# A decoder trunk on one Trainium2 core: four PSUM banks for the first sums of each MLP, separate tiles for the gate weights, and eight ways to begin a unit

## The chip, the cores and the metric

One core of one Trainium2 chip runs the whole program in one launch. The metric is the device time of that core in microseconds, from launch to end; smaller is better. Engine names are those of the profile: PE (matmul) with PEld (its weight loads), DVE (vector), ACT (scalar), POOL (GpSimd) and SP, whose queue issues all the DMAs.

## What is computed

Two layers over 256 tokens of width 2048. Layer 0 mixes by a gated linear recurrence, layer 1 by dilated attention; behind each stands an MLP with a squared ReLU. Every sublayer is normalized first and added to its input.

```python
for i in range(2):
    h = rmsnorm(x, mix_norm[i])
    if i == 0:
        x = x + rglru_block(h, w_in, conv_w, conv_b, w_a, b_a, w_x, b_x, lam, w_out)
    else:
        x = x + dilated_attention(h, w_qkv, w_o)
    h = rmsnorm(x, mlp_norm[i])
    x = x + square(relu(h @ w1[i])) @ w2[i]          # w1: 2048 x 8192, w2: 8192 x 2048
return rmsnorm(x, final_norm)

# rglru_block: xb, gb = split(h @ w_in); xb = causal conv of 4 taps
# r, i = sigmoid(block_diag(xb, w_a)), sigmoid(block_diag(xb, w_x))     10 blocks of 256 x 256
# a = exp(-8 r softplus(-lam)); h_t = a_t h_(t-1) + sqrt(1 - a_t^2) xb i; out = (h * gelu(gb)) @ w_out
```

All of it is float32, and the matmuls are done in fp32r: each operand is cut into a high part and the rest, and a product is three matmuls, high by high, high by low, low by high.

## The kernel before, in words

**Units.** The weights come in units of 128 x 2048 floats, 1 MB each (`unit`, L65), in one list. A DMA brings a unit into a `raw` tile (three buffers), ACT copies it to fp32r, which is its high part `whi` (`cut_hi`, L108; three buffers), and DVE subtracts to get `wlo` (`cut_lo`, L113; three buffers). The gates of the recurrence are units of half the width, 128 x 1024, in the same tiles. The tiles of one name are a ring: a new one takes the buffer of the third before it, and its writer waits until PE has read that.

**The order.** The work is a list of items, each the matmuls on one unit. The main loop (L916 to L926) runs it: before item `i` it issues loads up to unit `i+5`, `whi` up to `i+2` and `wlo` up to `i+2` (`before_unit`, L124); then come the item's matmuls, then `whi` of `i+3` (`behind_unit`, L130), and then what earlier items have asked for so many items later (`after`, L161): reading the sums, the next transposes, the activations. Each engine runs its own instructions strictly in this order.

**The recurrence.** For each of ten blocks there are four units of w_in, two for the recurrent branch and two for the other, and the gate unit of the block before, which stands behind the first of them; I call these five a turn. `stand_w` (L245) does a unit: sixteen slices of weights stand in PE and 256 tokens of `xT` move, three matmuls a slice: `whi` by the high tokens, `whi` by the low tokens, `wlo` by the high tokens. So a unit is 48 matmuls of 256 columns. Its sums go to a PSUM bank `acc` (four of them). `xb_done` reads them and runs the convolution on DVE, in block 1 partly on POOL; `conv_split` gives `chl`, the moving operand of the gate (`gate_run`, L373, 24 matmuls into two banks `g`); sigmoid, tanh, exp, square root, scan and split to `aT` follow over the next items.

**The MLP.** It goes by eight parts of 1024 hidden columns. The first matrix has eight units in a part, `j` = 0, 4, 1, 5, 2, 6, 3, 7 in this order, each done by `stand_w` into one of two banks `g`; `u_done` (L481) reads the bank on DVE with `rstdB`, the norm's factor, and the square and its split follow. For the second matrix the tokens and the columns are halved, and the product of a 2 x 2 block is done with seven products instead of eight, which is what the sums `qT`, `q` of weights and `sw`, `sT` of tokens are for. It works with 512 columns, in banks `acc` and `tr`. `ORDER` (L49) mixes the two: while part p has its second matrix, the units of part p+1 come in at the places "w", one between each two or three products, and `sums_of_tokens` runs behind each item.

**Part 0** has no part before it. `plan_start` does units 0 and 4 on the slices of the first three chunks of `xT`, and then on the fourth, since that is ready last; `plan_first` (L525) then does units 1, 5, 2, 6, 3, 7 on end. The factor `rstdB` takes longer: `rstd_rows` (L235) transposes it on PE behind unit 4, and ACT copies it, behind the `whi` that stand ahead of it.

Each layer is a scope with tiles of its own (`lru`); `wts`, `perm` and `psum` live through all of them.

Of the kernel before, what the change touches and what calls it, by code (L numbers as in the profile page):

```python
# [10 lines left out]
F32 = mybir.dt.float32  # L11
F32R = mybir.dt.float32r
# [5 lines left out]
S = 256  # L18
# [7 lines left out]
KD = D // 128  # L26
KR = DR // 128
NCH = D // 512
UW = 2048
# [12 lines left out]
HI_BUFS = 3  # L42
# [3 lines left out]
LOOK_LO = 2  # L46
LOOK_HI = 3
GROUPS = range(7)
ORDER = ("b11", "w", "b21", "s", "w", "t1", "w", "t2", "b22", "w", "s", "w", "t3", "w", "s", "w", "t4", "w", "s")  # L49


@with_exitstack
def trunk(ctx: ExitStack, tc: tile.TileContext, a: dict, out: bass.AP):
    nc = tc.nc
    P = 128

    perm = ctx.enter_context(tc.tile_pool(name="perm", bufs=1))
    wts = ctx.enter_context(tc.tile_pool(name="wts", bufs=1))
    psum = ctx.enter_context(tc.tile_pool(name="psum", bufs=1, space=bass.MemoryType.PSUM))
# [3 lines left out]
    units = []  # L63

    def unit(ap, width=UW):  # L65
        units.append({"ap": ap, "width": width})
        return len(units) - 1
# [6 lines left out]
    raw, split = {}, {}  # L74
# [14 lines left out]
    def make(i):  # L89
        if "load" in units[i]:  # L90
            units[i]["make"]()
            raw[i] = [(slice(0, UW), units[i]["source"]())]

    def new_hi(i):
        split[i] = (wts.tile([P, UW], F32R, name="whi", bufs=HI_BUFS),)

    def new_lo(i):
        split[i] += (wts.tile([P, UW], F32R, name="wlo", bufs=3),)

    def hi_piece(i, n):  # L100
        s, r = raw[i][n]
# [6 lines left out]
    def cut_hi(i):  # L108
        new_hi(i)
        for n in range(len(raw[i])):  # L110
            hi_piece(i, n)

    def cut_lo(i):  # L113
        new_lo(i)
        for n in range(len(raw[i])):
            lo_piece(i, n)
        del raw[i]
# [18 lines left out]
    def item(u, fn):  # L136
        items.append((u, fn))
# [21 lines left out]
    lru = Scope()  # L159

    def after(n, fn, *args):  # L161
        later.setdefault(now[0] + n, []).append((fn, args))

    def mm(o, l, r, start, stop):
        nc.tensor.matmul(o, l, r, start=start, stop=stop, skip_group_check=True)  # L165
# [23 lines left out]
    def xT(k):  # L189
        return state["xT", k // 4][:, k % 4, :]  # L190
# [51 lines left out]
        state["rstdB"] = rb  # L242


    def stand_w(ps, u, ks, w_at, first, last):  # L245
        hi, lo = split[u]
        for j, k in enumerate(ks):
            x = xT(k)
            s = slice((w_at + j) * 128, (w_at + j + 1) * 128)
            mm(ps, hi[:, s], x[:, 0:256], first and j == 0, False)  # L250
            mm(ps, hi[:, s], x[:, 256:512], False, False)
            mm(ps, lo[:, s], x[:, 0:256], False, last and j == len(ks) - 1)

    def stand_x(acc, u, get, ks, first, last, ts=range(NT)):
        hi, lo = split[u]
# [9 lines left out]
    def acc_tile():  # L265
        return psum.tile([P, 512], F32, name="acc", bufs=4)

    accs = {}
# [162 lines left out]
    def plan_rec():  # L431
        def proj(h, j, g):
            u = unit(a["w_in"][(KR if g else 0) + 2 * h + j])

            done = gb_done if g else xb_done
            if u < len(first):
                first[u] = (done, h, j)
                return

            def run():  # L440
                ps = acc_tile() if u > len(first) else psum.tile([P, 512], F32, name="g", bufs=2)
                stand_w(ps[:, :S], u, range(KD), 0, True, True)
                after(0, done, h, j, ps)
            item(u, run)
# [36 lines left out]
    def u_done(p, j, ps):  # L481
# [8 lines left out]
        after(1, u_low, t, uu)  # L490
        if h == 1 and p in GROUPS:
            after(1, waiting.append, (p, k))
# [31 lines left out]
    def plan_mlp(w1, w2, done):  # L524
        def plan_first(p, j):  # L525
            u = unit(w1[8 * p + j])

            def run():
                accs["u", p, j] = psum.tile([P, 512], F32, name="g", bufs=2)
                stand_w(accs["u", p, j][:, :S], u, range(KD), 0, True, True)  # L530
                after(0, u_done, p, j, accs.pop(("u", p, j)))
            item(u, run)

        def plan_start():
            us = [unit(w1[j]) for j in (0, 4)]
            for at, ks in enumerate((range(0, 12), range(12, 16))):
                for u, j in zip(us, (0, 4)):
                    def run(u=u, j=j, ks=ks, at=at):
                        if at == 0:
                            accs["u", 0, j] = psum.tile([P, 512], F32, name="g", bufs=2)  # L540
                        stand_w(accs["u", 0, j][:, :S], u, ks, ks[0], at == 0, at == 1)
                        if at == 1:
                            after(1 if j == 0 else 0, u_done, 0, j, accs.pop(("u", 0, j)))
                    item(u, run)
# [69 lines left out]
        for p in range(8):  # L614
            if p == 7 and done is final_done:
                item(None, load_g)
            if p < 7:
                nxt = iter([(p + 1, j) for j in (0, 4, 1, 5, 2, 6, 3, 7)])
            plain = [(n, h) for n in range(2 if p in GROUPS else 0, NCH) for h in range(2)]
            g = plan_group(p, 0) if p in GROUPS else {}  # L620
            for what in (ORDER if p in GROUPS else ("s", "w") * 8):
                if what == "w":
# [168 lines left out]
    first = [None] * 4  # L791
# [30 lines left out]
    for n in range(NCH):  # L822
        xg[n] = new_xg(n)
        rs = [wts.tile([P, UW], F32, name="raw", bufs=RAW_BUFS) for _ in range(3)] if n == 0 else rs
        for h in range(2 if n == 0 else 1):
            w = 2 if n == 0 else 4
            nc.sync.dma_start(xg[n][:, h * w:(h + 1) * w, :], a["xT"][:, 4 * n + h * w:4 * n + (h + 1) * w, :])
            for i in range(3):
                if n or i == 0:
                    s = slice(n * 512 + h * w * 128, n * 512 + (h + 1) * w * 128)  # L830
                elif h:
                    s = slice(0, 512)
# [5 lines left out]
        for h in range(2 if n == 0 else 1):  # L838
            w = 2 if n == 0 else 4
            for k in range(h * w, (h + 1) * w):  # L840
                nc.scalar.activation(t[:, k, 0:256], xg[n][:, k, :], AF.Identity, scale=pcol("mix0", 4 * n + k))
            for k in range(h * w, (h + 1) * w):
                nc.vector.scalar_tensor_tensor(t[:, k, 256:512], xg[n][:, k, :], pcol("mix0", 4 * n + k),  # L843
                                               t[:, k, 0:256].bitcast(F32), op0=OP.mult, op1=OP.subtract)
            for i in range(3):
                if n == 0 and h == 0:
                    new_hi(i)
                    new_lo(i)
                for at, (s, _) in enumerate(raw[i]):
                    if s.stop == n * 512 + (h + 1) * w * 128:  # L850
                        hi_piece(i, at)
                        lo_piece(i, at)
                        if s.start == 0:
                            accs["first", i] = acc_tile()
                            first[i] += (accs["first", i],)
                        ks = range(s.start // 128, s.stop // 128)
                        stand_w(accs["first", i][:, :S], i, ks, ks[0], s.start == 0, n == NCH - 1)
# [13 lines left out]
    for n in range(NCH):  # L871
        s = slice(n * 512, (n + 1) * 512)
# [15 lines left out]
    ps = psum.tile([P, 2, S], F32, name="tr", bufs=2)  # L888
# [23 lines left out]
    for at in range(len(items) - 1, -1, -1):  # L912
        u = items[at][0]
# [86 lines left out]
```

## Time and profile before

| | |
|---|---|
| time, median of 3 runs | 2189.44 us (2188.41 to 2190.64) |
| profiled execution, its own time | 2186.37 us |
| its span, first to last instruction | 2184.6 us |
| granted TensorE clock, mean | 0.995 |
| matmuls recorded | 13602 |
| read from HBM | 409.39 MB, 188 GB/s over the span |
| recurrence, MLP 0, attention, MLP 1 begin at | 5, 389, 1087, 1476 us |

A page gives each engine's busy time as a share of the span; matmuls are pipelined, and one record is longer than the distance to the next. So I read distances of starts. In a timeline a row is start, length, engine, line, operation, tiles written and read, shape, count, and in brackets the idle time before it and what ended it. In the list of waits a row is who waited for whom, total us, how many times, the longest. In the chain of waits a row is start, length and what the end of the program then hung on. Rows that group several instructions last from the first one's start to the last one's end.

### The profile page before, as it was taken

The numbers are of one execution on the slowest core, as the hardware profiler recorded it, in microseconds if no ns is written. First come the engines' busy times: TensorE is split into PE (matmuls) and PEld (weight loads), VectorE is DVE, ScalarE is ACT, GpSimd is POOL, SyncE is SP. The second block draws the span as 40 slices with busy tenths as digits, with TensorE's granted clock in tenths as the row PEclk, the third lists the DMA queues.
The fourth block names the chain that finished last, engine by engine and source line by source line (L and its number), as shares of the span: only waits on it lengthen the run. The fifth ranks groups of instructions, "written<-read, shape, count | busy, mean of one in ns | idle before, by whom it ended". The sixth has DMA issues, their size and how long they took to land.

```text
span 2184.6 us, 32102 instructions
## 1 busy us (share of the span) xinstructions
PE 2150.0 (98%) x13602; PEld 1944.2 (89%) x13602; DVE 1602.2 (73%) x1748; ACT 1166.2 (53%) x1261; POOL 81.3 (4%) x42
## 2 busy tenths in 40 slices
PE   7999999999999999999999999999999999999997
PEld 7999988999999999999888888889999999999996
DVE  8888865688888888787655555556888878887875
ACT  5777755554554555445545544555545544544543
POOL 2222100000000000000000000000000000000002
PEclk9999999999999999999999999999999999999999
DMA  6655565455465455554554444454564554545543
GB/s 220 213 190 190 183 222 180 174 203 221 138 248 189 177 195 207 185 223 163 179 198 156 172 174 173 157 191 161 206 231 144 222 213 154 218 187 193 212 175 134
DMA packets 61712, 413.56 MB, mean 189 GB/s; under 512 B 6784, under 2 KB 7168, under 8 KB 13440
## 3 DMA queue, kind: packets, MB, share of 16 engines
q1 hardware_dynamic: 61568, 411.51, 51.8%
q8 instruction: 106, 1.74, 0.3%
q14 instruction: 38, 0.31, 0.0%
HBM read 409.39 MB, written 2.10 MB: 188 GB/s over the span
## 4 chain that ended last, share of the span: by engine, by line
PE 80%; DVE 12%; ACT 5%; issue 2%; POOL 0%; DMA 0%; SPq 0%; DVEq 0%; ACTq 0%
PE acc L165 47%; PE g L165 27%; DVE wlo L106 7%; PE tr L165 4%; ACT whi L102 3%; DVE q L564 1%; ACT sT L181 1%; DVE xT L843 0%; DVE c L349 0%; DVE sT L182 0%; PE tr L205 0%; DVE aT L495 0%; DVE sw L506 0%; PE tr L664 0%; PE g L672 0%
## 5 line engine op out<-in xcount | busy, mean ns | idle before, releaser
L102 ACT ACTIVATE whi<-raw 128x2048 fp32r<-128x2048 f32 (+3 forms) x358 | 657.1, 1838 | 570.5 <-PE acc L165 313.9
L106 DVE TENSOR_TENSOR wlo<-raw,whi 128x2048 fp32r<-128x2048 f32 (+3 forms) x358 | 792.0, 2216 | 212.4 <-ACT whi L102 212.4
L165 PE MATMUL g<-xT,whi 128*128 128x256 f32 x4128 | 732.9, 281 | 5.8 <-DVE uu L486 5.8
L165 PEld LDWEIGHTS g<-xT,whi 128*128 128x128 f32 x4128 | 638.0, 188 | 15.2 <-DVE uu L486 6.3
L165 PE MATMUL g<-xT,wlo 128*128 128x256 f32 x2064 | 580.4, 281 | 2.1 <-DVE wlo L106 2.1
L165 PE MATMUL acc<-whi,aT 128*128 128x512 f32 x1840 | 580.5, 390 | 0.0
L165 PEld LDWEIGHTS acc<-whi,aT 128*128 128x128 f32 x1840 | 345.4, 188 | 69.6
L165 PEld LDWEIGHTS g<-xT,wlo 128*128 128x128 f32 x2064 | 395.3, 192 | 4.6 <-DVE wlo L106 4.6
L165 PE MATMUL acc<-wlo,aT 128*128 128x512 f32 x920 | 358.3, 389 | 0.0
L165 PE MATMUL acc<-whi,xT 128*128 128x512 f32 x768 | 245.9, 396 | 0.0
L165 PE MATMUL acc<-xT,whi 128*128 128x256 f32 x1248 | 223.5, 283 | 6.3 <-ACT whi L102 5.8
L165 PEld LDWEIGHTS acc<-wlo,aT 128*128 128x128 f32 x920 | 172.8, 188 | 33.5
L102 ACT ACTIVATE whi<-q 128x2048 fp32r<-128x2048 f32 x56 | 107.2, 1914 | 177.0 <-DVE q L564 137.8
L165 PEld LDWEIGHTS acc<-xT,whi 128*128 128x128 f32 x1248 | 195.0, 194 | 6.9 <-ACT whi L102 6.1
L165 PE MATMUL acc<-xT,wlo 128*128 128x256 f32 x624 | 178.2, 286 | 9.3 <-DVE wlo L106 9.0
L165 PEld LDWEIGHTS acc<-whi,xT 128*128 128x128 f32 x768 | 144.3, 188 | 30.7
L165 PE MATMUL acc<-wlo,xT 128*128 128x512 f32 x384 | 150.4, 392 | 0.0
L106 DVE TENSOR_TENSOR wlo<-q,whi 128x2048 fp32r<-128x2048 f32 x56 | 128.2, 2289 | 19.0 <-ACT whi L102 19.0
L165 PEld LDWEIGHTS acc<-xT,wlo 128*128 128x128 f32 x624 | 121.0, 194 | 12.0 <-DVE wlo L106 12.0
L102 ACT ACTIVATE whi<-qT 128x2048 fp32r<-128x2048 f32 x28 | 53.7, 1916 | 132.7 <-DVE qT L564 132.7
L106 DVE TENSOR_TENSOR wlo<-qT,whi 128x2048 fp32r<-128x2048 f32 x28 | 64.2, 2293 | 47.8 <-ACT whi L102 47.8
L165 PEld LDWEIGHTS acc<-wlo,xT 128*128 128x128 f32 x384 | 72.2, 188 | 15.1
(172 smaller groups left out, 1917.3 us busy)
## 6 DMA issues: line engine op xcount, KB each, us to landing
raw<-in_w SPq DMA_DIRECT2D x214, 1024.0 KB, 4.8
raw<-in_w_qkv SPq DMA_DIRECT2D x48, 1024.0 KB, 4.8
q<-in_w SPq DMA_DIRECT2D x42, 1024.0 KB, 6.9
raw<-in_w_in SPq DMA_DIRECT2D x35, 1024.0 KB, 4.8
raw<-in_w_out SPq DMA_DIRECT2D x20, 1024.0 KB, 4.8
raw<-in_w_o SPq DMA_DIRECT2D x16, 1024.0 KB, 4.8
raw<-in_w_g SPq DMA_DIRECT2D x10, 512.0 KB, 3.5
raw<-in_w_in SPq DMA_DIRECT2D x11, 256.0 KB, 6.1
```

The lines of the kernel that those rows point to most:

```text
L102: nc.scalar.activation(split[i][0][:, s], r, AF.Copy)
L106: nc.vector.tensor_sub(split[i][1][:, s], r, split[i][0][:, s].bitcast(F32))
L165: nc.tensor.matmul(o, l, r, start=start, stop=stop, skip_group_check=True)
L181: nc.scalar.activation(hi_out, src, AF.Copy)
L564: nc.vector.tensor_add(q[to], q[a], q[b])
```

## The change

Three things.

First, in part 0 of each MLP the sums of all eight units go to the four banks `acc` instead of the two banks `g`. The other parts keep `g`.

Second, the gates' halves have tiles of their own, `ghi` and `glo`, 128 x 1024, two buffers each, in the layer's own pool. `whi` and `wlo` keep three buffers each, which the gates no longer use.

Third, `stand_w` takes a way to begin, and `plan_first` picks it by `j`. A tuple of widths cuts the unit's first matmul (high weights by high tokens) into so many pieces of these widths, each a matmul with the same weights; "low" puts `wlo` by the high tokens first in every slice; "other" begins the unit with the low tokens and takes the high ones second. `plan_start` passes none, so units 0 and 4 of part 0 begin as before.

```diff
+BEGIN = {0: (), 4: (128, 128), 1: (64, 192), 5: (192, 64), 2: (32, 224), 6: (64, 64, 128), 3: "low", 7: "other"}
...
+    def cut_tile(i, name, bufs):
+        width = units[i].get("width", UW)
+        if width < UW:
+            return lru.tile([P, width], F32R, name="g" + name, bufs=2)
+        return wts.tile([P, UW], F32R, name="w" + name, bufs=bufs)
+
     def new_hi(i):
-        split[i] = (wts.tile([P, UW], F32R, name="whi", bufs=HI_BUFS),)
+        split[i] = (cut_tile(i, "hi", HI_BUFS),)
...
-    def stand_w(ps, u, ks, w_at, first, last):
+    def stand_w(ps, u, ks, w_at, first, last, begin=()):
+
         hi, lo = split[u]
         for j, k in enumerate(ks):
             x = xT(k)
             s = slice((w_at + j) * 128, (w_at + j + 1) * 128)
-            mm(ps, hi[:, s], x[:, 0:256], first and j == 0, False)
-            mm(ps, hi[:, s], x[:, 256:512], False, False)
-            mm(ps, lo[:, s], x[:, 0:256], False, last and j == len(ks) - 1)
+            parts = [(hi, 0, 0, 256), (hi, 0, 256, 512), (lo, 0, 0, 256)]
+            if begin == "low":
+                parts = parts[2:] + parts[:2]
+            elif begin == "other" and j == 0:
+                parts = [parts[1], parts[0], parts[2]]
+            elif begin and j == 0:
+                at, cuts = 0, []
+                for n in begin:
+                    cuts.append((hi, at, at, at + n))
+                    at += n
+                parts = cuts + parts[1:]
+            for n, (w, o, c0, c1) in enumerate(parts):
+                opens = first and j == 0 and n == 0
+                mm(ps[:, o:o + c1 - c0], w[:, s], x[:, c0:c1], opens, last and j == len(ks) - 1 and n == 2)
...
-                accs["u", p, j] = psum.tile([P, 512], F32, name="g", bufs=2)
-                stand_w(accs["u", p, j][:, :S], u, range(KD), 0, True, True)
+                accs["u", p, j] = acc_tile() if p == 0 else psum.tile([P, 512], F32, name="g", bufs=2)
+                stand_w(accs["u", p, j][:, :S], u, range(KD), 0, True, True, BEGIN[j])
...
-                            accs["u", 0, j] = psum.tile([P, 512], F32, name="g", bufs=2)
+                            accs["u", 0, j] = acc_tile()
```

On PE, at the end of unit 4 of part 0 and the start of unit 1, the rows were these (`tr<-con,rs` are the transposes of the norm's factor, the rows below them unit 1):

```order
L165 MATMUL g<-xT_4024,whi 128x256 x2
L165 MATMUL g<-xT_4024,wlo 128x256
L238 MATMUL tr<-con,rs 128x128 x2
L165 MATMUL g<-xT_3601,whi 128x256 x2
L165 MATMUL g<-xT_3601,wlo 128x256
L165 MATMUL g<-xT_3601,whi 128x256 x2
L165 MATMUL g<-xT_3601,wlo 128x256
```

They are now these, in the numbering of the changed file:

```order
L173 MATMUL acc<-xT_4024,whi 128x256 x2
L173 MATMUL acc<-xT_4024,wlo 128x256
L246 MATMUL tr<-con,rs 128x128 x2
L173 MATMUL acc<-xT_3601,whi 128x64
L173 MATMUL acc<-xT_3601,whi 128x192
L173 MATMUL acc<-xT_3601,whi 128x256
L173 MATMUL acc<-xT_3601,wlo 128x256
L173 MATMUL acc<-xT_3601,whi 128x256 x2
L173 MATMUL acc<-xT_3601,wlo 128x256
```

The bank is another, and the first matmul of unit 1 is two, of 64 and 192 columns. Nothing else moved on PE but such pieces, and the order of the three matmuls in units 3 and 7.

On ACT, in a turn of the recurrence, with the semaphores that each row waits for (`whi<-raw` are the high parts of coming units, the ACT_TABLE_LOAD and `r<-g` open the gate's sigmoid), it was:

```order
L102 ACTIVATE whi<-raw 128x2048 [waits DMAHW6_49,PE_49]
L181 ACTIVATE aT_2351<-i 128x256 [waits DVE_49]
L181 ACTIVATE aT_2354<-i 128x256
L368 ACTIVATE gw<-gb 128x512 [waits DVE_49,Pool_49]
L102 ACTIVATE whi<-raw 128x2048 [waits DMAHW7_49,PE_49,Activation_49]
L392 ACT_TABLE_LOAD
L392 ACTIVATE r<-g,par 128x256 x2
```

And now:

```order
L110 ACTIVATE whi<-raw 128x2048 [waits DMAHW6_49,PE_49]
L189 ACTIVATE aT_2351<-i 128x256 [waits DVE_49]
L189 ACTIVATE aT_2354<-i 128x256
L388 ACTIVATE gw<-gb 128x512 [waits DVE_49,Pool_49]
L110 ACTIVATE whi<-raw 128x2048 [waits DMAHW7_49,PE_49]
L412 ACT_TABLE_LOAD [waits PE_49]
L412 ACTIVATE r<-g,par 128x256 [waits Activation_49]
```

The instructions and their order are the same on ACT, DVE, POOL and SP. What moved is the waiting: both `whi` shown still wait for PE, but each for the end of the unit one before, since the gate no longer stands in their ring; and the wait for the gate's own end now stands at the table load behind the second `whi`. The `ghi` of a gate waits for its DMA alone.

More of the change, by code (lines that the diff above doesn't have):

```diff
@@ L92, in make @@
             raw[i] = [(slice(0, UW), units[i]["source"]())]
+    def cut_tile(i, name, bufs):
[3 more added lines that the diff above has]
+        return wts.tile([P, UW], F32R, name="w" + name, bufs=bufs)
     def new_hi(i):
-        split[i] = (wts.tile([P, UW], F32R, name="whi", bufs=HI_BUFS),)
+        split[i] = (cut_tile(i, "hi", HI_BUFS),)
     def new_lo(i):
-        split[i] += (wts.tile([P, UW], F32R, name="wlo", bufs=3),)
+        split[i] += (cut_tile(i, "lo", 3),)
     def hi_piece(i, n):
```

## The prediction

> **What bounds the kernel now.** I read the page first: the span, and which engine is busy all the time.
>
> ```profile
> span 2184.6 us, 32102 instructions
> PE 2150.0 (98%) x13602; PEld 1944.2 (89%) x13602; DVE 1602.2 (73%) x1748; ACT 1166.2 (53%) x1261; POOL 81.3 (4%) x42
> ```
>
> PE is the bound, so time goes only where PE waits or where its matmuls come slower than they could. The list of waits of PE says what the waits are worth:
>
> ```profile
> PE acc L165 <- DVE wlo L106: 9.0, 9, 3.1
> PE g L165 <- DVE uu L486: 5.8, 2, 2.9
> PE g L165 <- DVE wlo L106: 2.1, 12, 0.2
> ```
>
> All waits together are some 23 us, 1%. The second figure is how often. The two on uu stand at the start of part 0 of each MLP; PE's timeline there:
>
> ```profile
> 400.99 0.38 PE L238 MATMUL tr<-con,rs 128*128 128x128 f32 x2
> 404.29 0.50 PE L165 MATMUL g<-xT,whi 128*128 128x256 f32 x2 [2.91 <-DVE uu L486]
> 1488.30 0.38 PE L238 MATMUL tr<-con,rs 128*128 128x128 f32 x2
> 1491.60 0.50 PE L165 MATMUL g<-xT,whi 128*128 128x256 f32 x2 [2.92 <-DVE uu L486]
> 1492.11 0.63 PE L165 MATMUL g<-xT,whi 128*128 128x256 f32 x2
> 1495.31 0.43 PE L165 MATMUL g<-xT,whi 128*128 128x256 f32 x2
> ```
>
> The third unit wants a bank of `g`, both are held by units 0 and 4, and these are read only when rstdB is there. From 1492.11 to 1495.31 fifteen matmuls take 3.20 us, 0.213 each, half the usual pace: PE came back cold. After the first MLP's wait it did not.
>
> The second thing is pace. The chain of waits, with stretches of the same kind of matmul:
>
> ```profile
> 136.45 16.39 PE acc L165 x142
> 237.12 16.99 PE acc L165 x142
> 404.29 32.93 PE g L165 x288
> 484.33 5.55 PE g L165 x47
> 489.90 1.93 ACT whi L102
> 491.85 2.29 DVE wlo L106
> 496.84 2.28 DVE wlo L106
> 510.24 2.30 DVE wlo L106
> 512.58 5.50 PE g L165 x46
> 685.18 5.68 PE g L165 x46
> ```
>
> The same 142 matmuls take 16.39 or 16.99 us: there is a quick and a slow pace, 4.2 ns a matmul apart, 0.20 us on a unit of 48. A stretch keeps its pace. The last two rows are the same unit of two parts, each behind a wait, one quick, one slow; so how a unit begins decides, and I cannot see by which rule. Nearly all units between 512-column work are slow, as at 484.33 (5.55 for 47; the quick 32.93 for 288 is 5.37 for 47).
>
> The same rows show that from 489.90 to 512.58 the chain is not PE's: it runs over ACT and DVE from the end of unit 2 to the `wlo` of unit 7, where PE waits:
>
> ```profile
> 512.00 0.40 PE L165 MATMUL g<-xT,whi 128*128 128x256 f32 x2
> 512.58 0.38 PE L165 MATMUL g<-xT,wlo 128*128 128x256 f32 x1 [0.18 <-DVE wlo L106]
> ```
>
> The third matmul would have started at 512.24 (two at 0.118), and starts 0.34 later. What units 6 and 3 gain or lose up to 0.34 is therefore hidden.
>
> **Part 0 in four banks.** Unit 1 no longer waits for uu; it starts when the two transposes are through, 0.25 us behind 400.99 and 1488.30: 404.29 - 401.24 and 1491.60 - 1488.55, 3.05 each, -6.1. Its weights are there. Unit 5 is next late:
>
> ```profile
> 399.66 3.71 ACT L102 ACTIVATE whi<-raw 128x2048 fp32r<-128x2048 f32 x2 [1.30 <-PE g L165]
> 401.61 2.29 DVE L106 TENSOR_TENSOR wlo<-raw,whi 128x2048 fp32r<-128x2048 f32 x1 [2.27 <-ACT whi L102]
> ```
>
> Those are its halves (DVE, then 403.90), wanted at 401.24 + 5.65 = 406.9: 3.0 us to spare. Banks: units 1 and 5 take those that the last w_out chunk has left, unit 2 that of unit 0, read by 404.29 (that is what the wait was for) and wanted at 401.24 + 2 x 5.65 = 412.5. The cold stretch goes with the wait: fifteen matmuls at 0.213 instead of 0.114, -1.5. The Trainium skill, page "TensorE: Matmul & The Clock Gate", section "What's actually happening", lets the clock halve after an idle window that runs free of the kernel; by that rule either, both or neither wait could find it, and this profile has one of two. The credit for the timed runs is thus 0 to 3.0. On the other side, the six units behind the wait ran quick; if half of them are slow now, that is six times 0.20, +1.2. Five more matmuls per part 0 come in (below), +1.1.
>
> **Gate tiles of their own.** In the first stage PE waits once a turn on `wlo`:
>
> ```profile
> 110.60 0.39 PE L165 MATMUL acc<-xT,whi 128*128 128x256 f32 x2
> 111.29 0.39 PE L165 MATMUL acc<-xT,wlo 128*128 128x256 f32 x1 [0.29 <-DVE wlo L106]
> 111.51 0.40 PE L165 MATMUL acc<-xT,whi 128*128 128x256 f32 x2
> 102.43 1.92 ACT L102 ACTIVATE whi<-raw 128x2048 fp32r<-128x2048 f32 x1 [3.52 <-PE acc L165]
> 104.68 0.76 DVE L182 TENSOR_TENSOR aT<-i,aT 128x256 fp32r<-128x256 f32 x2 [1.82 <-ACT aT L181]
> 108.95 5.58 DVE L106 TENSOR_TENSOR wlo<-raw,whi 128x2048 fp32r<-128x2048 f32 x2
> PE acc L165 <- DVE wlo L106: 1.8, 6, 0.3
> ```
>
> (PE, ACT, DVE, and PE's waits from 110 to 270.) The matmul at 111.29 was due at 110.83, and the next came 0.22 behind it instead of 0.11: 0.57 lost. It goes back to ACT at 102.43, which waited for a whi buffer until its unit had ended; aT stood behind it on ACT, DVE waited 1.82 for aT, and the `wlo` at 108.95 came that much late. When the gate takes none of the three buffers, this `whi` waits for the unit before: 3.52 us go at its head, DVE's 1.82 with them, and the first of the two `wlo` runs from 107.13 to 109.4, 1.4 before it is wanted. DVE is next late, but in time. Six waits at 0.57: -3.4. The wait of 2.4 us near 81 stays: ACT there stands behind the Pool engine, which the change leaves alone.
>
> ```profile
> PE acc L165 <- DVE wlo L106: 2.4, 1, 2.4
> 63.29 0.63 ACT L181 ACTIVATE chl<-c 128x512 fp32r<-128x512 f32 x1 [4.76 <-POOL c L347]
> ```
>
> The wait for the gate's end moves to the table load in front of the sigmoid, which needed it anyway.
>
> **The beginnings.** Cutting adds one matmul to units 4, 1, 5, 2 and two to unit 6; 94 in all. No fp32r matmul under 256 columns is in the trace. Two neighbours bound its price:
>
> ```profile
> 393.05 1.04 PE L205 MATMUL tr<-con,xc 128*128 128x128 f32 x8
> 393.84 0.48 PE L165 MATMUL g<-xT,whi 128*128 128x256 f32 x2
> 1162.89 0.39 PE L671 MATMUL g<-qk 128*128 128x128 f32 x2
> 1163.12 0.60 PE L672 MATMUL g<-qk 128*128 128x256 f32 x2
> 1163.55 0.49 PE L695 MATMUL tr<-con,s 128*128 128x128 f32 x3
> ```
>
> Eight transposes of 128 columns need 0.79, 0.10 each, though half as wide as 256: each has its weight load. Two pieces for one matmul then cost 2 x 0.10 - 0.118 = 0.08 more, or 0.118 if a piece is no cheaper than the whole; I take 0.11. Fp32 matmuls, two records each, take 0.23 for 128 and 0.43 for 256 columns. If narrow fp32r went at that rate, an opening of 256 columns would cost 0.43 instead of 0.118, +0.31 a unit. Nothing rules out a gain either, since the opening may bring the quick pace (-0.20). I take the transposes: like these matmuls they are one record each. On the path stand, in 14 parts, units 4, 1, 5, 2: 56 x 0.11 = +6.2, and half of them quick, 28 x -0.20 = -5.6. Units 6 (0.22), 3 and 7 lie under the 0.34; if that cover is gone, 14 x 0.22 = 3.1. Unit 3 wants `wlo` first: that is the one of 496.84, ready at 499.1; by PE's order unit 3 starts behind unit 6 and 24 matmuls of 512 columns, 13 us after 490, so it has some 4 us to spare. The Trainium skill, same page, section "Back-to-back issue gap", gives 81 ns for a pair of load and matmul at 128 columns; the transposes here need 100. By 81 the 66 pieces on the path cost 5.3 instead of 7.3, and the sum would be 2 us lower.
>
> **Sum.** -6.1 - 1.5 + 1.2 + 1.1 - 3.4 + 6.2 - 5.6 = -8.1. The profiled execution took 2186.37 (span 2184.6 and 1.8 around it), 3.1 below the median of 2189.44; I carry the difference over: 2189.44 - 8.1 = **2181.3**. Its own range, with the cold credit at 0 to 3.0 and a quarter to three quarters of the units quick (2.8 either way): 2176 to 2186.
>
> **Rivals.**
> - Narrow fp32r pieces run at the fp32 rate. Then 56 + 8 units cost 0.31 instead of pieces at 0.11: 19.8 instead of 7.3, sum +4.4, 2193.8; with no unit turned quick (+5.6) 2199.4. It decides from 0.24 us a unit on: without the pieces the sum is -15.4, over 64 units. For it: the L671 and L672 rows, the only ones with as few columns that are no transposes. Against: at 256 columns fp32r (0.118) is not run the fp32 way (0.43), and no row says that it is below. Chance 0.28, half of it slower by more than can be told from no change.
> - The first stage loses its quick pace. Its waits also reset it: 136.45 was quick behind one, 237.12 slow. Without waits it keeps what it has after 89 us: seven turns of 192 matmuls slow, 7 x 192 x 0.0042 = +5.6, sum -2.5, 2186.9. Chance 0.18.
> - No beginning turns a unit quick: +5.6 and +1.2 in part 0, sum -1.3, 2188.1. Chance 0.12. All do: -5.6 - 1.2, 2174.5, chance 0.06.
> - The gate tiles do not do what they are for: DVE itself is late and the six waits stay. Sum -4.7, 2184.7. Chance 0.06.
>
> **Numbers.** The forecast has 0.30. A measurement of this kernel tells about 0.2% (4.4 us) from no change. Faster by more: 0.28 of the forecast, 0.06 of all quick, 0.03 of the gate tiles, 0.03 of the first rival, 0.08 of the slow first stage and of no unit quick: 0.48. Slower by more: 0.14 of the first rival, and 0.06 for its mixtures with a slow first stage: 0.20. The rest, 0.32. The range takes in all quick nearly and the first rival up to its upper half: 2174 to 2198.
>
> **What would show it.** In the profile after: no wait on uu in the list; the chain's 404.29 row starting near 401; the six `wlo` waits after 105 us gone, and the rows of 142 still 16.4; the starts of a unit 4 or 1 cut, 0.11 and not 0.2 to 0.4 apart; units of 48 at 5.45 or 5.65 by their place, the same in all parts. It is wrong if narrow pieces take more than twice 0.118, if uu or a bank of `acc` still holds unit 1, or if a new wait stands at unit 5 or 2 of part 0.

## The result and the profile after

| | before | after |
|---|---|---|
| time, median of 3 runs | 2189.44 us (2188.41 to 2190.64) | 2174.44 us (2173.93 to 2174.55) |
| ratio, 95% interval | | 0.9932 (0.9913 to 0.9952) |
| profiled execution, its own time | 2186.37 us | 2173.93 us |

15.0 us less, where 8.1 had been forecast: the sign is right and the size half. The page after, span and engines, and the list of PE's waits, its first two rows (only one more, of 1.3, is over a microsecond):

```profile
span 2172.1 us, 32279 instructions
PE 2143.5 (99%) x13696; PEld 1938.4 (89%) x13696; DVE 1601.9 (74%) x1748; ACT 1168.5 (54%) x1261; POOL 80.6 (4%) x42
```

```profile
PE acc L173 <- DVE wlo L114: 8.1, 4, 2.7
PE acc L173 <- ACT whi L110: 6.3, 2, 5.8
```

PE issues 94 matmuls more and is busy 6.5 us less, so its matmuls come quicker. The 5.8 us on uu are gone, and of the nine waits on `wlo` into `acc` four are left. The start of part 0 of the first MLP, PE's timeline (the row of three is the piece of 64, the one of 192 and the next matmul of 256):

```profile
395.07 0.38 PE L246 MATMUL tr<-con,rs 128*128 128x128 f32 x2
395.21 0.59 PE L173 MATMUL acc<-xT,whi 128*128 128x64 f32 x3
395.64 0.28 PE L173 MATMUL acc<-xT,wlo 128*128 128x256 f32 x1
```

Unit 1 begins 0.14 us behind the transposes, where it had stood 3.3 behind them. The chain of waits, so that the stages can be set side by side; first five rows of before at the stages' borders (the first full turn, the recurrence's last stretch, unit 0 of part 1 and the last unit of part 7 of the first MLP, unit 0 of part 1 of the second), then after:

```profile
84.47 18.04 PE acc L165 x142
282.09 49.32 PE acc L165 x216
439.95 5.65 PE g L165 x48
1030.30 5.65 PE g L165 x48
1528.85 5.65 PE g L165 x48
```

```profile
82.88 17.99 PE acc L173 x142
...
103.73 21.77 PE acc L173 x192
125.50 2.87 PE g L173 x24
128.37 21.77 PE acc L173 x192
...
276.18 49.31 PE acc L173 x216
395.45 33.27 PE acc L173 x293
431.45 5.65 PE g L173 x48
445.27 5.56 PE g L173 x49
453.56 5.76 PE g L173 x49
...
503.97 5.49 PE g L173 x46
590.15 5.69 PE g L173 x46
1021.71 5.65 PE g L173 x48
1516.09 5.65 PE g L173 x48
```

Each border read against its counterpart of before gives what the stage in front of it saved:

| stage | border before, after | saved | forecast |
|---|---|---|---|
| start | 84.47, 82.88 | 1.6 | 0 |
| turns of the recurrence | 282.09, 276.18 | 4.3 | 3.4 |
| first MLP to the end of part 0 | 439.95, 431.45 | 2.6 | half of 5.3 |
| its parts 1 to 7 | 1030.30, 1021.71 | 0.1 | -0.3 |
| attention, second MLP to the end of part 0 | 1528.85, 1516.09 | 4.2 | half of 5.3 |
| its parts 1 to 7, end | 2184.6, 2172.1 | -0.3 | -0.3 |

In the recurrence the stretch is no longer broken: gate (24) and units (192) follow one another, and a turn is 24.64 us (128.37 - 103.73), not 25.17. In the MLP's parts the rows from 431.45 on are units 0, 4, 1 of a part, uncut 5.65, (128,128) 5.56, (64,192) 5.76, and then unit 7 of two parts behind its wait, quick (5.49 for 46) and slow (5.69). Parts 1 to 7 together gain nothing.

The 1.6 us at the start are put down to chance, not to the change. The chain has there, in this profile and in the one of the same kernel run again (below), these rows of the first units, which wait for what the DMAs bring:

```profile
30.62 6.86 PE acc L173 x58
```

```profile
30.03 8.46 PE acc L173 x58
```

The border that stands at 82.88 here lay between 81.3 and 84.7 us in the eight profiles with banks and gate tiles, and between 83.1 and 85.5 in the five others; so most of the 1.6 is chance, and that all of it is can't be told. Taken so, profile against profile the change is worth 12.4 - 1.6 = 10.8 us, and the medians are 15.0 apart. The kernel before scatters more: on one chip 15 of its runs lay between 2181.0 and 2192.1, five of the changed one between 2173.4 and 2174.9 (five more, at another time, between 2169.6 and 2173.7).

### The profile page after: what moved, and what is told of

Same layout as the page of the kernel before. It is cut to its first block, busy times and chain, and to the rows that moved or that the text cites. A ratio compares the mean times of both kernels' runs of the same rounds, so it can differ in the third digit from the quotient of the medians.

```text
span 2172.1 us, 32279 instructions
## 1 busy us (share of the span) xinstructions
PE 2143.5 (99%) x13696; PEld 1938.4 (89%) x13696; DVE 1601.9 (74%) x1748; ACT 1168.5 (54%) x1261; POOL 80.6 (4%) x42
## 4 chain that ended last, share of the span: by engine, by line
PE 83%; DVE 10%; ACT 4%; issue 1%; DMA 0%; POOL 0%; SPq 0%; DVEq 0%; ACTq 0%
PE acc L173 53%; PE g L173 24%; DVE wlo L114 6%; PE tr L173 4%; ACT whi L110 2%; DVE q L584 1%; ACT sT L189 1%; DVE sT L190 0%; PE tr L213 0%; DVE aT L515 0%; DVE sw L526 0%; PE tr L684 0%; PE g L692 0%; DVE xT L863 0%; DVE sw L528 0%
## 5 line engine op out<-in xcount | busy, mean ns | idle before, releaser
L110 ACT ACTIVATE whi<-raw 128x2048 fp32r<-128x2048 f32 (+2 forms) x348 | 647.2, 1862 | 561.5 <-PE acc L173 346.1
L114 DVE TENSOR_TENSOR wlo<-raw,whi 128x2048 fp32r<-128x2048 f32 (+2 forms) x348 | 780.9, 2248 | 214.4 <-ACT whi L110 210.7
L173 PE MATMUL g<-xT,whi 128*128 128x256 f32 (+3 forms) x3700 | 642.5, 278 | 0.0
L173 PEld LDWEIGHTS g<-xT,whi 128*128 128x128 f32 x3700 | 567.0, 189 | 8.2
L173 PE MATMUL g<-xT,wlo 128*128 128x256 f32 x1808 | 505.0, 279 | 1.5
L173 PEld LDWEIGHTS g<-xT,wlo 128*128 128x128 f32 x1808 | 340.8, 188 | 4.5 <-DVE wlo L114 4.0
L173 PE MATMUL acc<-xT,whi 128*128 128x256 f32 x1770 | 307.8, 279 | 7.7 <-ACT whi L110 6.3
L173 PEld LDWEIGHTS acc<-xT,whi 128*128 128x128 f32 x1770 | 269.9, 190 | 8.8 <-ACT whi L110 6.6
L173 PE MATMUL acc<-xT,wlo 128*128 128x256 f32 x880 | 245.7, 280 | 8.3 <-DVE wlo L114 8.1
L173 PEld LDWEIGHTS acc<-xT,wlo 128*128 128x128 f32 x880 | 166.8, 190 | 9.6 <-DVE wlo L114 9.4
```

Source lines behind the costliest of these rows:

```text
L110: nc.scalar.activation(split[i][0][:, s], r, AF.Copy)
L114: nc.vector.tensor_sub(split[i][1][:, s], r, split[i][0][:, s].bitcast(F32))
```

## The experiments

Theory A: the gain is that of the waits, in part 0 and in the recurrence, with the half-speed stretch and the slow stretches that came behind them; the ways to begin give about nothing, because a cut costs the time of one full matmul and wins that back only where it leaves the unit at the quick pace. The rival B: the beginnings carry the 7 us that the forecast missed (the number came out as that of its rival in which all units turn quick, 2174.5).

**The parts of the change one by one.** Banks alone, gate tiles alone, the two together and the changed kernel again were timed on one chip beside 15 runs of the kernel before (2188.54), the high half alone and the beginnings alone on another beside 21 runs of it (2185.72); ratios have their 95% interval.

*Four banks alone.* The kernel before with

```diff
-                accs["u", p, j] = psum.tile([P, 512], F32, name="g", bufs=2)
+                accs["u", p, j] = acc_tile() if p == 0 else psum.tile([P, 512], F32, name="g", bufs=2)
...
-                            accs["u", 0, j] = psum.tile([P, 512], F32, name="g", bufs=2)
+                            accs["u", 0, j] = acc_tile()
```

> The kernel before with only the four banks in part 0 of each MLP; no unit begins in another way and the gates stay in the common tiles. Theory A (the gain is the waits: in the two profiled executions part 0 of the two MLPs is 2.6 and 4.1 us shorter, beginnings included): 6 to 9 us faster, the upper end where both waits came back cold in the timed runs; 5 if the six units behind the wait fall back to 117.8 ns a matmul. Theory B (the beginnings carry most of what the forecast missed): 3.05 twice and little more, 4 to 6 us faster, with the six units slow.

Measured: 2179.94 us, 8.6 less, ratio 0.9958 (0.9945 to 0.9970). Its chain at the six units of part 0, first and second MLP:

```profile
402.29 33.92 PE acc L165 x288
1487.66 32.66 PE acc L165 x288
```

No wait on uu and no half-speed stretch in part 0, one MLP slow (117.8 ns a matmul) and one quick (113.4), from the same code. 8.6 lies at the upper end of A, and outside B.

*Gate tiles alone.* The kernel before with `cut_tile` and the tiles it makes.

> The kernel before with only the gates' tiles of their own. Theory A: seven turns at 24.63 instead of 25.17 us and one slow stretch less, 4.4 us faster, the six waits on wlo gone. Theory C (the two us by which the start is shorter in the profile after belong to the change, through the tiles' places): 6 us faster, and the first row of 58 matmuls of the chain again 6.86 long instead of 8.47.

Measured: 2183.51 us, 5.0 less, ratio 0.9978 (0.9969 to 0.9988). PE's waits on `wlo` into `acc`, the first wait on uu with what came behind it in the timeline, and two windows with the granted clock (the column PEclk, third from the end), ahead of the wait and behind it:

```profile
PE acc L171 <- DVE wlo L112: 8.1, 4, 2.7
```

```profile
399.12 0.80 PE L171 MATMUL g<-xT,whi 128*128 128x256 f32 x2 [2.91 <-DVE uu L492]
...
399.93 0.63 PE L171 MATMUL g<-xT,whi 128*128 128x256 f32 x2
...
400.57 0.63 PE L171 MATMUL g<-xT,whi 128*128 128x256 f32 x2
```

```profile
390.00:395.00 5.00, 5.00 (x44) 5.00 (x44) 2.44 (x9) 3.23 (x9) 0.00 (x0) 1.00 0.43 182
399.00:402.00 3.00, 2.88 (x13) 2.88 (x14) 3.00 (x5) 1.56 (x4) 0.00 (x0) 0.50 0.70 227
```

The waits in the recurrence go as theory A says, and the first 58 matmuls take 7.10 here, so C, by which the start belongs to the change, had one number on its side; it fell with the 8.46 above. The half speed is the clock: granted 1.00, and 0.50 behind the wait, three matmuls in 0.64 us (399.93 to 400.57) instead of 0.34. It came in the first MLP here, in the second in the profile before. In the profiles of the four kernels that keep the wait (before, gate tiles alone, their high half alone, beginnings alone) it came behind five of eight such waits, and cost some 1.3 to 2.8 us each time (2.8 here: the six units behind the wait took 35.75 us, and 32.93 in the first MLP of before, at the same quick pace without it). The Trainium skill, page "TensorE: Matmul & The Clock Gate", section "What's actually happening", has the window of idleness run free of the kernel; that only some of eight waits of the same 2.9 us were followed by it agrees, but the page gives that window about 3.4 us, and the waits here are shorter. The changed kernel is not rid of the half clock: its wait on `wlo` in the first stage (2.61 us, ended at 82.88) stays, and behind that wait, of 2.3 to 2.6 us, ten of the thirteen profiles were granted 0.50 for some microseconds, before and after alike.

*The high half of the gate alone in a tile of its own.* Against the kernel with both tiles:

```diff
-        split[i] += (cut_tile(i, "lo", 3),)
+        split[i] += (wts.tile([P, UW], F32R, name="wlo", bufs=3),)
```

> The kernel before with a tile of its own for the high half of the gates alone; the low half stays in the common ring of wlo. Theory H (what held DVE was the whi that waited for a buffer): the six waits go as with both tiles, 4 to 5 us faster. Theory L (the low half in the ring of wlo holds it too): the six waits stay, 0 to 1 us.

Measured: 2182.92 beside 2185.72 of before (21 runs), 2.8 less, ratio 0.9989 (0.9980 to 0.9998). The chain's turns:

```profile
102.66 2.82 PE g L171 x24
...
127.26 2.82 PE g L171 x24
```

The stretch is unbroken as with both tiles: 24.60 us a turn, so H holds in the trace, and the ring of `whi` was the cause. The gain is less than H gave, though the time is that of both tiles (2183.51, on the other chip, where the kernel before took 2.8 more); this profile has the half clock behind both waits on uu, which the edit leaves, and whether the timed runs had it as often is open.

*Beginnings alone.* The changed kernel with `g` in part 0 and the gates in the common tiles.

> The kernel before with the ways to begin alone; part 0 keeps two banks and its wait, the gates the common tiles. Behind part 0 three units of five on the path gain 0.09, one loses 0.11, and unit 7 is more often slow behind its wait: within 1 us of the kernel before; in part 0 five pieces more at 0.11 and no pace to win where the units behind the wait were quick, so in all 1 us faster to 2 slower. By the theory that the beginnings carry the gain, 5 to 7 faster.

Measured: 2184.86 beside 2185.72, ratio 0.9998 (0.9988 to 1.0008). Nothing, as A says; B is out.

*Banks and gate tiles without beginnings*, and *the changed kernel again*, on the chip of the first two:

```diff
-                stand_w(accs["u", p, j][:, :S], u, range(KD), 0, True, True, BEGIN[j])
+                stand_w(accs["u", p, j][:, :S], u, range(KD), 0, True, True)
```

> The changed kernel with no unit beginning in another way: banks and gate tiles alone. Theory A: as quick as the changed kernel, within 1.5 us, since in the parts behind part 0 the changed kernel's profile gains only 0.1 us in 590; the units of 48 at 5.65, and unit 7 behind its wait mostly quick again. Theory B: 5 to 7 us slower than the changed kernel, 8 to 10 faster than the kernel before.

> The changed kernel once more, beside the three others on one chip. All theories: 12 to 16 us faster than the kernel before; it is the mark against which the run without the beginnings is read.

Measured: 2173.58 (2171.68 to 2175.64), ratio 0.9931 (0.9918 to 0.9943), and 2174.21 (2173.37 to 2174.89), ratio 0.9933 (0.9920 to 0.9945). The beginnings are worth nothing that can be told. Banks (8.6) and gate tiles (5.0) sum to 13.6, the two together give 15.0: they hardly touch.

**Why the beginnings give nothing: one way in each part.** `WAYS` by MLP and part takes the place of `BEGIN[j]` behind part 0:

```diff
+WAYS = (((128, 128), (64, 192), (192, 64), (32, 224), (64, 64, 128), "other", "low"),
+        ((224, 32), (96, 160), (160, 96), (128, 64, 64), (64, 64, 64, 64), (64, 128, 64), ()))
...
+                stand_w(accs["u", p, j][:, :S], u, range(KD), 0, True, True, BEGIN[j] if p == 0 else WAYS[layer][p - 1])
```

> The changed kernel, but behind part 0 all eight units of a part begin in one way, another in each part: first MLP parts 1 to 7 (128,128), (64,192), (192,64), (32,224), (64,64,128), other, low; second MLP (224,32), (96,160), (160,96), (128,64,64), (64,64,64,64), (64,128,64), uncut. Theory W (the way decides): behind a stretch of 512 columns a way gives the same pace at every place of its part: (128,128), (192,64), (32,224) and (64,64,128) 113.3 ns a matmul, units of 5.56, with three pieces 5.68; (64,192), other, low and uncut 117.8, units of 5.65 or 5.76. Theory P (the place decides): units 1, 0 and 3 slow whatever the cut, 4, 5, 2, 6 quick whatever the cut. For the second MLP's ways theory W gives no pace, only that it is one pace a part.

From one profiled execution, the chain's rows for units 0 and 4 of the first way and unit 0 of the next six, and then unit 0 of (224,32), (160,96) and (64,64,64,64) of the second MLP:

```profile
432.12 5.56 PE g L175 x49
445.85 5.56 PE g L175 x49
...
518.19 5.76 PE g L175 x49
...
605.30 5.56 PE g L175 x49
...
691.36 5.57 PE g L175 x49
...
777.54 5.68 PE g L175 x50
...
864.04 5.65 PE g L175 x48
...
950.34 5.65 PE g L175 x48
```

```profile
1516.97 5.76 PE g L175 x49
...
1691.23 5.76 PE g L175 x49
...
1865.06 5.79 PE g L175 x51
```

The way decides, not the place: all units of a part that have no wait in them have one length, and theory W's numbers stand. 5.56 for 49, 5.68 for 50 and 5.79 for 51 are 113.5 ns a matmul; 5.65 for 48 and 5.76 for 49 are 117.6 to 117.7. Of the two-piece cuts (128,128), (192,64), (32,224) lead into the quick pace, (64,192), (224,32), (96,160), (160,96) do not; of those with three or four pieces all that were tried do. By which rule I can't say. So each piece costs as much as a full matmul, 0.11, and a good way gives 0.20: 0.09 a unit is left, a bad one loses 0.11.

**What a narrow matmul costs.** The third matmul of every slice narrowed in the first MLP (the kernel leaves out the rest of that product there), the first of every slice cut in the second.

```diff
+            if isinstance(begin, int):
+                parts[2] = (lo, 0, 0, begin)
...
-            elif begin and j == 0:
+            elif begin and (every or j == 0):
```

> Measures a narrow matmul by itself. Behind part 0 of the first MLP the third matmul of every slice takes 32, 64, 96, 128, 160, 192 and 224 columns in parts 1 to 7 (the rest of low weights by high tokens is left out there); in the second MLP the first matmul of every slice, not only of the first, is cut: (128,128), (64,192), (192,64), (32,224), (64,64,128), (64,64,64,64), (64,128,64). Theory L (each matmul takes a full turn of about 0.113, however narrow): units of the first MLP 5.4 to 5.7 at every width; in the second 16 x 0.113 longer a piece, 7.25 to 7.5 with two, 9.1 with three, 10.9 with four. Theory C (columns decide, 0.113 x n / 256): the first MLP's units 1.6 shorter at 32, 0.9 at 128, 0.2 at 224; the second's no longer than 5.45 to 5.65. Theory F (the rate of fp32, 0.23 for 128): units of the second 16 x 0.31 longer or more, over 10.

From one profiled execution, the chain, unit 0 with 32 and 224 columns, and then with two and four pieces in every slice:

```profile
432.39 5.45 PE g L175 x48
...
948.78 5.54 PE g L175 x48
...
1514.63 7.35 PE g L175 x64
...
2028.01 10.94 PE g L175 x96
```

Theory L: 16 matmuls seven times narrower save 0.09 us in a unit, where C wanted 1.4 between 224 and 32 columns, and 32 pieces more cost 3.6 (10.94 - 7.35). A matmul takes 0.114 to 0.115 on the mean, with narrow ones among them or not. Sixteen matmuls of 256 cut into two of 128 make a unit 1.7 longer (7.35 against 5.65), not 5.0 (16 x 0.31), as the fp32 rate would: F is out. The Trainium skill, same page, section "Back-to-back issue gap", gives 81 ns for a pair of load and matmul at 128 columns; here it is 115 on the mean of a unit in which half of the matmuls are that narrow (7.35 / 64), and the measurement decides.

**A version that beats both.** Only quick ways, and only where the path is:

```diff
+def begin_of(p, j):
+    if p == 0:
+        return (64, 192) if j == 1 else ()
+    return (192, 64) if p == 7 or j in (0, 4, 1, 5, 2) else ()
```

> Banks and gate tiles as in the changed kernel, but the way to begin is chosen by what the run with a way a part showed: behind part 0 units 0, 4, 1, 5, 2 begin with (192,64), units 6, 3, 7 uncut (they lie under the chain that ends at unit 7), in part 7 all eight (192,64); in part 0 only unit 1 is cut, (64,192). If a cut costs 0.11 and (192,64) turns a unit quick at every place: five units at 5.56 instead of 5.65, 0.47 a part, 12 parts, two parts with eight, and four pieces fewer in each part 0: 7 us faster than the run without beginnings, 6 to 8 faster than the changed kernel, 20 to 22 faster than the kernel before. If the gain is taken back at unit 7, whose wait ends at the same distance behind unit 2 but may leave it slow: 2 to 3 less.

Measured: 2168.12 us (2167.32 to 2169.30) beside 2185.72, ratio 0.9923 (0.9909 to 0.9936). That is 17.6 less, not the 20 to 22 that were expected; the kernel before took 2185.72 here and 2188.54 on the first chip. Against the changed kernel's 2174.21, of another set, it is 6.1, inside the 6 to 8 expected. Once more, beside the changed kernel on one chip:

> The kernel with (192,64) at units 0, 4, 1, 5, 2 once more, beside the changed kernel on one chip, since the kernel before scatters by 9 us and the two had been timed in different calls. If 2168.1 against 2174.2 holds: 5.3 to 6.1 us quicker than the changed kernel, the two ranges apart. If it was the chip: within 1 us.

> The changed kernel, the mark for the run beside it: 2173 to 2175 us.

Measured: 2165.76 (2164.66 to 2168.36), ratio 0.9909 (0.9895 to 0.9923), against 2172.68 (2169.57 to 2173.69), ratio 0.9938 (0.9924 to 0.9951). 6.9 us quicker than the changed kernel, the two ranges of times apart, and a little more than the 5.3 to 6.1 expected; the changed kernel itself lies just under its 2173 to 2175. Its chain, the six units of both parts 0 and unit 1 of the first MLP's part 1, which the changed kernel leaves at 5.76:

```profile
397.09 32.77 PE acc L178 x289
...
454.62 5.56 PE g L178 x49
...
1478.08 32.77 PE acc L178 x289
```

## Why the prediction was right or wrong

**Part 0.** The waits were worth what was put down, and no new wait stands at units 5 and 2. The cold stretch was taken at 1.5 each; the five seen cost 1.3 to 2.8. "Half of the six units slow" was too dark: with unit 1 cut as (64,192) all were quick in every profile of the changed kernel (33.27 for 293), while uncut one MLP came out slow and one quick. That is 1.2; with it the two parts 0 save 6.8 in the profile, not 5.3. Why (64,192) is quick behind the transposes and slow behind 512 columns is open.

**The gates.** The mechanism held: the ring of `whi`, the wait at aT, six waits, and the wait near 81 still there (2.61 us, now at 82.88). 4.3 came out instead of 3.4: 0.6 of the difference is the slow stretch of before (16.99 against 16.39), which went too, and 0.3 isn't assigned. So the rival "the first stage loses its quick pace" had it the wrong way round, and its step "without waits it keeps what it has" is refuted. Two chains, of the run with one way a part and of the banks alone:

```profile
103.66 22.50 PE acc L175 x192
126.16 2.86 PE g L175 x24
129.02 21.77 PE acc L175 x192
```

```profile
110.69 16.99 PE acc L165 x142
136.46 16.38 PE acc L165 x142
```

In the first, with the gate tiles, a turn does go slow: it begins quick, three matmuls in 0.34 us, and from 109.17, where the next unit's first `wlo` matmul starts, it takes 0.35 to the end. The gate's 24 matmuls behind it, at 0.119 each, hand over to the quick pace again. All other full turns behind a gate were quick in the profiles of the kernels that have the tiles, but for the same one of the run on widths (22.52). In the second, with the waits, each turn draws its pace anew.

**The beginnings.** The price, 0.11 a piece, was right, and the rival of the fp32 rate is dead. "Half of them quick" came out as three ways of four, and for a reason the forecast did not have: the way decides, the same in all parts. By the sum that is 56 x 0.11 - 42 x 0.20 = -2.2 instead of +0.6. The profile shows +0.2 over the 14 parts. A part with unit 7 quick in both profiles is 86.19 us instead of 86.30, 0.11 less and not 0.16, so some 1.5 came in; but unit 7, behind its wait, was quick in 1 of 12 parts and had been in 9 before, 8 x 0.20 = 1.6. This is chance and not its way: the same kernel had 9 and 12 of 12 in its two other profiles. The cover held: units 6 and 3 cost nothing, and unit 7 still waits.

**The sum.** Profile against profile 12.4 us went, of which 1.6 at the start is taken as chance: 10.8 against 8.1. The miss is 1.5 in part 0, 0.9 in the gates, 0.4 in the beginnings. **The step that failed** most is the last one: "I carry the difference over". The median of before lay 3.1 above its profiled execution, the median after 0.5 above: 2.6 of the 15.0 was extra time of the three timed runs of before. Part of it is the draw of these three (2188.4 to 2190.6): larger sets of the same kernel have medians of 2188.54 (15 runs), 2186.05 (9) and 2185.72 (21), around the profiled 2186.37, and the changed kernel, timed again beside the first two, was 14.3 and 13.4 us quicker. Shown is that the kernel before scatters more, and that banks and gate tiles, each alone, gain more in timed runs (8.6 and 5.0) than was forecast. Argued, not shown, is of what the extra time is made: what varied from profile to profile is the half clock (1.3 to 2.8 each time), the pace of the six units (1.2 each) and of the turns (0.6 each), and the prediction let only the half clock vary from run to run, as 0 to 3.0.

That the time lies in the stated range at all, 2174 to 2198, is luck: the forecast's own range began at 2176, and the lower end was put at 2174 for a rival that did not come true. 2174.44 is not that rival "all turn quick" at 2174.5: unit 1 stayed slow in all 14 parts, and without any way to begin the time is the same.

## What to carry to other kernels

A wait of PE can cost more than its length: what comes behind it may run at half clock or at a slow pace for a whole stretch, by chance from run to run, and a single profile shows only one draw of it. The scatter went down with the waits here (eleven runs each spread over 7.0 us with all the waits and the beginnings, over 4.8 and 4.1 without those of the recurrence), though what made it is not shown. Time the kernel before often enough: its median moved by 2.8 us between the two largest sets. Price a matmul by its issue, not its columns, before cutting one. Where a stream has two paces, measure each way of entering it once, all in one kernel, and use a quick one only on units that are on the path.

## What the runs showed of the hardware

- Streams of fp32r matmuls with a 128 x 128 weight load each took 0.114 to 0.115 us a matmul on the mean, with narrow ones from 32 columns up among those of 256 (5.45 us for 48 with every third at 32; 10.94 for 96 with two thirds at 64).
- A stream of 256 columns ran at one of two paces, 113.5 or 117.7 ns a matmul. How a unit behind 512-column work begins sets it: each of fourteen ways gave one pace at every place where nothing waited.
- The gate's 24 matmuls took 2.80 us from the common tiles, 2.87 from tiles of their own and 2.82 with only the high half in one; in the profiles the last two were followed by the quick pace. What in the tiles' places does this is open.
- The granted clock fell to 0.50 behind five of eight waits of PE of 2.9 us in the MLPs, and behind ten of thirteen of 2.3 to 2.6 us in the first stage.
